# Mixer products cut at half a tile, more buffers in three pools, and a new work list for two transformer layers

## The chip, the core and the metric

The kernel runs on one core of a Trainium2 chip. TensorE (PE) multiplies matrices, VectorE (DVE), ScalarE (ACT) and GpSimd (POOL) work on vectors, and SyncE (SP) issues the transfers. Each engine takes its instructions in a fixed order. The metric is the device time of the whole program in microseconds (us), lower is better.

## What is computed

Two layers of a diffusion backbone run over 512 latent tokens of width 1024, with 256 context tokens in front of them. Each layer has a mixer with three groups of heads (attention, retention, a state space recurrence called SSD) and an MLP with squared ReLU; only the latent tokens are the output, so layer 1 leaves out the context rows where it can.

```python
def trunk_layer(x, xc, mod, mod_c, norm_g, w_in, w_out, ...):
    h = rmsnorm(x, norm_g[0]) * (1 + sc1[:, None]) + sh1[:, None]
    qa, ka, va, qr, kr, vr, gr, z, xbc, dt = jnp.split(h @ w_in, split_idx, axis=-1)
    att, att_c = attention_mixer(...)          # 6 query heads, 2 key heads, rotary
    ret, ret_c = retention_mixer(...)          # 4 heads, both directions, group norm, silu gate
    ssd, ssd_c = ssd_mixer(...)                # conv of 5 taps, silu, 6 heads, both directions, gated norm
    o = jnp.concatenate([att, ret, ssd], axis=-1) @ w_out
    x = x + g1[:, None] * rmsnorm(o, norm_g[1])
    h2 = rmsnorm(x, norm_g[2]) * (1 + sc2[:, None]) + sh2[:, None]
    x = x + g2[:, None] * rmsnorm(jnp.square(jax.nn.relu(h2 @ w1)) @ w2, norm_g[3])
    return x, xc
```

## The kernel before

Tokens stand in six tiles of 128 (four latent, two of context), and the model width in KC = 8 blocks of 128. Every large product is made of three matmuls (`mm3`): each operand is kept as a high part, rounded to the matmul's type, and a low part, the rest. So a weight piece (`wunit`) is loaded into a raw buffer `wr`, ACT writes its high part `wh` and DVE or POOL the low part `wl` (line 344); `h_h` and `h_l` (lines 570 and 571) are the same for the normed input, with POOL or DVE for `h_l`.

A layer runs in this order: the input norm, the convolution of xbc with SSD behind it, attention, retention, the output product, and the FF product, which is over half of the time. Layer 1's first input tiles are normed at the end of layer 0's FF (the layer boundary): `sandwich` scales the FF result (`tt`, `ors`, `xt`, lines 1489 to 1496), `norm_tile` transposes (`nps`) and modulates it; there POOL makes `h_l` and the low part of the first xbc weights, `wl_xbc`.

The mixers are written as some 250 named units, and `PLAN[l]` is a list of their names by hand; the loop at line 1414 calls them in that order. A scheduler then orders each engine's instructions by it, and by when buffers come free. The names: `kv` is the key, value and dt projection and `kp` its norm and rotary; `xw`, `xa`, `xb`, `xc`, `xt` are weight, first product, second product, taps and transposes of one of seven column blocks of the convolution; `qa`, `zz`, `kr`, `qg` are the other four projections, one unit a token tile; `f`, `m`, `b`, `g`, `sv`, `si`, `sd` belong to SSD (its `b` makes yi, for which POOL's `tb` is an input, and its `f` the product F from DVE's `gfb`); `as`, `at`, `ao` are attention's scores, transposes of P and products pv. In retention, of head h, `rl` loads the duplicated q and k (`ddqr`, `ddkr`), `rp` transposes them, `rx` centres v (`centre_v`), `rs` makes scores, `rd` the state sums, `rt` the states `rst` on DVE, `ro` the products `ry`, `rg` the gain on POOL, `rn` the group norm; `ur`, `us`, `ua` transpose the finished head groups into the mixer output (`sT`), and `wo` starts the output product (`op`) with the head groups that are ready.

Buffers: `t3` has four buffers and holds cin, acc and th of the convolution and other short-lived tiles, `m6` has three, the staging tiles `st` three. In the convolution ACT copies the product out of PSUM into `cin` (line 842), makes the first tap `acc` (line 850), DVE adds four taps (line 852), ACT takes the tanh `th` (line 854) and DVE the last product (line 861). POOL clears the edges of `cin` (lines 832 to 835) and, for qa, makes `wl_qa`. The gain tiles and `ry` of retention share two `m6` buffers, which `ret_y` takes once all of attention's products are done.

## Time and profile before

| what | value |
| --- | --- |
| median of 3 runs | 1861.27 us (1858.37 to 1863.56) |
| the profiled execution's own time | 1859.15 us |
| its span, first to last instruction | 1857.4 us |
| mean granted clock of TensorE | 0.972 |
| busy: PE, DVE, ACT, POOL | 1752.8, 1207.3, 703.0, 370.4 us |

Times in the views count from the span's start. A busy time is the sum of an engine's instructions; the idle time of PE in a stretch is the stretch less its busy time. PEclk is the granted clock as a share of 2.4 GHz, so 0.5 is 1.2 GHz. `[2.00 <-DMA ddqr]` behind a row says that the engine sat idle for 2.00 us before it and what ended that. "x4" merges four instructions in a row. In layer 0 the mixer takes the time from about 43 to 450 us, the output product that to 546 and FF that to 1088; layer 1's mixer runs from 1114 to 1447, and its FF from 1511 to the end.

### The profile page before, as it was taken

The page shows a single profiled execution, that of the slowest core. Times are in us where ns is not written, and L with a number is a line of the kernel's source. Part 1 is how long each engine was busy: PE and PEld are TensorE (multiplying, and loading weights), DVE is VectorE, ACT ScalarE, POOL GpSimd, SP SyncE. Part 2 cuts the span into 40 slices and gives each one's busy share as a digit, 9 for nine tenths or more (in the row PEclk, how much of TensorE's full clock was granted, in tenths as well). Part 3 has the DMA queues.
Part 4 walks back from the last instruction along what each step waited for, and adds up shares of the span by engine and source line. Part 5 has one row for each costly group of instructions (what it writes and reads, how often), then busy time and mean ns, then how long its engine had stood idle before and what let it go on. Part 6 is the DMA issues. An engine that isn't in the chain of part 4 may idle for free. (4 is left out here: it accounts for less than half of the span.)

```text
span 1857.4 us, 24648 instructions
## 1 busy us (share of the span) xinstructions
PE 1752.8 (94%) x8991; PEld 1440.8 (78%) x8991; DVE 1207.3 (65%) x2462; ACT 703.0 (38%) x1267; POOL 370.4 (20%) x391
## 2 busy tenths in 40 slices
PE   7998999998999999999999979899988999999998
PEld 2887977646878888888888878787767788888886
DVE  5878875776667566667556678788766644444445
ACT  6544376743551211211211475445751632222222
POOL 0047222313000100100100132543122011111112
PEclk9999999999999999999999989999985999999999
DMA  8420443466434434434434433133342522223332
GB/s 278 125 58 27 127 120 105 125 193 176 160 130 121 147 91 125 136 107 121 130 98 125 143 120 109 54 102 112 92 119 54 171 102 91 91 92 101 98 106 92
DMA packets 189077, 217.00 MB, mean 117 GB/s; under 512 B 67666, under 2 KB 142236, under 8 KB 188956
## 3 DMA queue, kind: packets, MB, share of 16 engines
q1 hardware_dynamic: 188956, 215.43, 38.9%
q8 instruction: 71, 1.16, 0.3%
q14 instruction: 50, 0.41, 0.1%
HBM read 189.66 MB, written 25.72 MB: 116 GB/s over the span
## 5 line engine op out<-in xcount | busy, mean ns | idle before, releaser
L589 PE MATMUL f<-h_h,wh_f 128*128 128x512 f32 (+1 forms) x800 | 280.6, 351 | 1.4 <-ACT h_h L570 1.4
L591 PE MATMUL f<-h_h,wl_f 128*128 128x512 f32 (+1 forms) x800 | 281.7, 352 | 0.0
L590 PE MATMUL f<-h_l,wh_f 128*128 128x512 f32 (+1 forms) x800 | 280.9, 351 | 0.8 <-DVE h_l L571 0.8
L1558 POOL TENSOR_TENSOR r<-r 128x768 f32<-128x768 f32 (+1 forms) x64 | 95.7, 1496 | 841.1 <-ACT r L1557 734.3
L589 PE MATMUL f<-wh_g,uh 128*128 128x512 f32 x640 | 252.7, 395 | 2.5 <-DVE uh L1559 1.6
L590 PE MATMUL f<-wl_g,uh 128*128 128x512 f32 x640 | 252.5, 395 | 0.0
L591 PE MATMUL f<-wh_g,ul 128*128 128x512 f32 x640 | 251.8, 393 | 0.0
L343 ACT ACTIVATE wh_f<-wr_f 128x1024 fp32r<-128x1024 f32 x64 | 66.5, 1055 | 374.5 <-PE f L591 133.1
L1588 DVE TENSOR_TENSOR acc<-acc,f 128x512 f32<-128x512 f32 x140 | 96.1, 686 | 121.0 <-PE f L591 119.6
L589 PEld LDWEIGHTS f<-h_h,wh_f 128*128 128x128 f32 x800 | 152.4, 191 | 23.1 <-ACT h_h L570 1.5
L590 PEld LDWEIGHTS f<-h_l,wh_f 128*128 128x128 f32 x800 | 151.6, 190 | 22.9 <-DVE h_l L571 1.0
L591 PEld LDWEIGHTS f<-h_h,wl_f 128*128 128x128 f32 x800 | 151.8, 190 | 20.8
L527 DVE SCALAR_TENSOR_TENSOR ga<-wr_mg,cg_a,ga 128x512 f32<-128x512 f32 x216 | 151.2, 752 | 12.5 <-DMA wr_mg<-in_w_mod_dram 12.4
L589 PEld LDWEIGHTS f<-wh_g,uh 128*128 128x128 f32 x640 | 120.1, 188 | 31.5 <-DVE uh L1559 2.1
L591 PEld LDWEIGHTS f<-wh_g,ul 128*128 128x128 f32 x640 | 120.2, 188 | 28.6
L590 PEld LDWEIGHTS f<-wl_g,uh 128*128 128x128 f32 x640 | 120.2, 188 | 27.3
L1557 ACT ACTIVATE r<-f 128x768 f32<-128x768 f32 (+1 forms) x64 | 44.6, 697 | 193.5 <-PE f L591 126.6
L1559 DVE CAST uh<-r 128x768 fp32r<-128x768 f32 (+1 forms) x64 | 32.4, 506 | 126.3 <-POOL r L1558 126.3
L344 DVE TENSOR_TENSOR wl_f<-wr_f,wh_f 128x1024 fp32r<-128x1024 f32 x64 | 77.6, 1221 | 50.8 <-ACT wh_f L343 50.7
L344 DVE TENSOR_TENSOR wl_g<-wr_g,wh_g 128x1024 fp32r<-128x1024 f32 x62 | 75.4, 1222 | 51.4 <-ACT wh_g L343 51.4
L343 ACT ACTIVATE wh_g<-wr_g 128x1024 fp32r<-128x1024 f32 x64 | 67.3, 1056 | 94.2 <-DMA wr_g<-in_w_ff_dram 55.5
L589 PE MATMUL xbc<-h_h,wh_xbc 128*128 128x512 f32 (+1 forms) x208 | 71.9, 346 | 3.9 <-ACT cin L842 3.9
(405 smaller groups left out, 3762.2 us busy)
## 6 DMA issues: line engine op xcount, KB each, us to landing
wr_f<-in_w_ff_dram SPq DMA_DIRECT2D x64, 512.0 KB
wr_g<-in_w_ff_dram SPq DMA_DIRECT2D x64, 512.0 KB
wr_mg<-in_w_mod_dram SPq DMA_DIRECT2D x192, 128.0 KB
wr_m<-in_w_mod_dram SPq DMA_DIRECT2D x24, 512.0 KB
m<-in_w_mod_dram SPq DMA_DIRECT2D x32, 256.0 KB
wr_o<-in_w_out_dram SPq DMA_DIRECT2D x16, 512.0 KB
wr_xbc<-in_w_in_dram SPq DMA_DIRECT2D x14, 512.0 KB
xmid<-xt SPq DMA_DIRECT2D x10, 512.0 KB
```

The lines of the kernel that those rows point to most:

```text
L343: S.activation(hv[:, a0 : a0 + an], r, AF.Copy)
L344: (lo_eng or V).tensor_tensor(lv[:, a0 : a0 + an], r, hv[:, a0 : a0 + an].bitcast(F32), ALU.subtract)
L527: V.scalar_tensor_tensor(acc[:, s], r2[:, k % 2], w, acc[:, s], ALU.mult, ALU.add)
L589: T.matmul(o, a[0], b[0], start=first, stop=False)
L590: T.matmul(o, a[0], b[1], start=False, stop=False)
L591: T.matmul(o, a[1], b[0], start=False, stop=last)
L1557: S.activation(r, q[:, :NT], AF.Relu)
L1558: G.tensor_tensor(r, r, r, ALU.mult)
L1559: V.tensor_copy(uh, r)
L1588: V.tensor_tensor(acc[tt][:, ns], acc[tt][:, ns], qs[tt][half], ALU.add)
```

## The change

The products of `xa`, `qa`, `zz`, `kr` and `qg` are divided into two units at KC/2 (`xa3.` and `xa3`). The scratch of the dynamic DMAs is set to 2048 bytes a partition; `t3` goes from four to six buffers, `m6` and `st` from three to four. `ret_y` is gone: `ry` and the gain tiles are t3 tiles. `rv` (the load of v for retention) depends on `kr5` alone. `wo` has nine units for six, and a unit `wq` loads another weight piece for them. Low parts move: of the eight `wl_qa` and of the two `wl_xbc` of the boundary from POOL to DVE, of the last but one `h_l` there too, of one attention put (`ua2`) a layer and of one modulation piece, and one skip product a layer. Three modulate operations of a tile go from DVE to ACT (CUT). Both lists are new; of them the diff shows the first rows of layer 1's.

```diff
-ATT_N9 = True
+ATT_N9 = False
+KNOBS = dict(
+    H_LO="GGGGVV", KV_LATE=1, X_LO="VVVVVVVV", W_LO="VVVVVVVV", P_MUL="VSVSVS", SKIP="VVGVGV",
+    U_LO="GGV", MOD="GGGVGG", T3=6, M6=4, S1=3, ST=4, CUT="443444",
+)
...
     1: """
-        kv0 kv1 kv2 kv3 kv4 kv5 km0 km1 xw3 xa3 xb3 xa4 xc3 xb4 xt3 xc4 xw5 xa5 kp1 xc5 de xa6 xt4
...
+        kv0 kv1 kv2 kv3 kv4 kv5 km0 km1 xw3 xa3. xa3 xb3 xa4. xa4 xb4 xc3 xt3 xw5 xa6. xa5. xc4 kp1 xa5 xt4 de
...
-        modulate(q, xh.rearrange("p (k t) -> p k t", k=KC), tt, l, which, hT, lo_eng)
+        modulate(q, xh.rearrange("p (k t) -> p k t", k=KC), tt, l, which, hT, lo_eng, (0, KC), int(KNOBS["CUT"][tt]))
...
-        t3 = lambda shape, name, dt=F32: mp.tile(shape, dt, tag="t3", name=f"{name}{l}", bufs=4)
+        t3 = lambda shape, name, dt=F32: mp.tile(shape, dt, tag="t3", name=f"{name}{l}", bufs=KNOBS["T3"])
-        m6 = lambda shape, name, dt=F32: mp.tile(shape, dt, tag="m6", name=f"{name}{l}", bufs=3)
+        m6 = lambda shape, name, dt=F32: mp.tile(shape, dt, tag="m6", name=f"{name}{l}", bufs=KNOBS["M6"])
...
-        def tm_group(name, n, cols, nt, consume, banks=(pB,), us=None):
-            us = us or [wunit(wcols(w_in[l], 4 * u, cols), (128, 4, n), f"{name}{l}{u}", G if name == "qa" else None) for u in range(2)]
+        def tm_group(name, n, cols, nt, consume, banks=(pB,), us=None, split=False):
+            us = us or [wunit(wcols(w_in[l], 4 * u, cols), (128, 4, n), f"{name}{l}{u}", eng(KNOBS["W_LO"][4 * l + ("qa", "zz", "kr", "qg").index(name)]) if not us else None) for u in range(2)]
...
+                    if split and k == KC // 2 - 1:
+                        yield
...
+                if k == KC // 2 - 1 and part == 0:
+                    yield
...
-            for t in range(nt):
-                unit(f"{nm}{t}", steps(gen), f"{nm}{t - 1}" if t else "kv5")
+            for t in range(nt):
+                unit(f"{nm}{t}.", steps(gen), f"{nm}{t - 1}" if t else None)
+                unit(f"{nm}{t}", steps(gen), f"{nm}{t}.")
...
-        def ret_y():
-            RV["y"] = [m6([128, 1536], f"ry{i}") for i in range(2)]
...
-                ry[pr] = RV["y"][pr][:, :768].rearrange("p (t h d) -> p t h d", t=6, h=2)
+                ry[pr] = t3([128, 6, 2, 64], f"ry{pr}")
...
-            a, b = (RV["y"][h % 2][:, c : c + 384].rearrange("p (t d) -> p t d", d=64)[:, :NQ] for c in (768, 1152))
+            ab = t3([128, 2, 6, 64], f"gg{h}")
+            a, b = ab[:, 0, :NQ], ab[:, 1, :NQ]
...
-        unit("rv", ret_v, "kr5", *[f"at{h}{t}" for h in range(6) for t in range(NQ)])
-        unit("ryt", ret_y, *[f"ao{h}{t}" for h in range(6) for t in range(NQ // 2)])
+        unit("rv", ret_v, "kr5")
...
-            WP["g"] = wout_begin(l, MX["m"], WP["p"], 6)
+            WP["g"] = wout_begin(l, MX["m"], WP["p"], 9)
+
+        def wo_more():
+            WP["p"][0][1, 1] = wout_unit(l, 1, 1)
...
-                    kvw.append(xbc_unit(l + 1, (3, 4), G))
+                    kvw.append(xbc_unit(l + 1, (3, 4), eng(KNOBS["X_LO"][4])))
...
-    nc = bacc.Bacc("TRN2", target_bir_lowering=False, num_devices=1)
+    nc = bacc.Bacc("TRN2", target_bir_lowering=False, num_devices=1, dynamic_dma_scratch_size=2048)
```

On DVE, at the layer boundary, where `xt` of one tile is followed by the modulate operations of the next (lines of the changed kernel are about 54 lower). Before:

```order
L1491 TENSOR_TENSOR tt_9702<-acc05_5369,gr011_9611 128x512
L299 SCALAR_TENSOR_TENSOR rm_t_9557<-nrs_9554,rm_h_9556 128x1
L299 SCALAR_TENSOR_TENSOR rm_t_9625<-ors_9618,rm_h_9624 128x1
L303 SCALAR_TENSOR_TENSOR nrs_9554<-rm_t_9557,nrs_9554 128x1
L303 SCALAR_TENSOR_TENSOR ors_9618<-rm_t_9625,ors_9618 128x1
L1495 SCALAR_TENSOR_TENSOR xt_9613<-tt_9614,ors_9618,xt_9613 128x1024
L1492 TENSOR_TENSOR oss_9705<-oss_9705 128x1
```

After:

```order
L233 SCALAR_TENSOR_TENSOR rm_t_9629<-ors_9622,rm_h_9628 128x1
L233 SCALAR_TENSOR_TENSOR rm_t_9561<-nrs_9558,rm_h_9560 128x1
L237 SCALAR_TENSOR_TENSOR ors_9622<-rm_t_9629,ors_9622 128x1
L1437 TENSOR_TENSOR tt_9706<-acc05_5373,gr011_9615 128x512
L237 SCALAR_TENSOR_TENSOR nrs_9558<-rm_t_9561,nrs_9558 128x1
L1441 SCALAR_TENSOR_TENSOR xt_9617<-tt_9618,ors_9622,xt_9617 128x1024
L278 TENSOR_TENSOR wl_xbc13_9696<-wr_xbc13_0_9697,wh_xbc13_9695 128x1024
L278 TENSOR_TENSOR wl_xbc13_9696<-wr_xbc13_4_9701,wh_xbc13_9695 128x1024
```

The two `wl_xbc`, which POOL made before, stand behind `xt`.

On PE, at the end of layer 1's attention, from its last pv on. Before:

```order
L1176 MATMUL pv151_12584<-PT5101_12547,vat1_11263 128x256 x6
L1176 MATMUL pv151_12584<-PT5111_12548,vat1_11263 128x256 x6
L274 MATMUL dTqr01_12621<-ident_69,ddqr01_12606 128x128 x4
L1280 MATMUL rd10_12666<-vrr1_12603,W01_12477 128x64 x6
L1273 MATMUL rs100_12688<-qT01_12627,kT01_12626 128x128 x4
L274 MATMUL dTkr11_12646<-ident_69,ddkr11_12639 128x128 x4
L1304 MATMUL ry10_12711<-vrr1_12603,W01_12477 128x64
L274 MATMUL dTqr11_12651<-ident_69,ddqr11_12640 128x128 x4
L1305 MATMUL ry10_12711<-rst10_12694,q201_12628 128x64
L1304 MATMUL ry10_12711<-vrr1_12603,W01_12477 128x64
```

After, from one row earlier:

```order
L208 MATMUL pt1531_12586<-ident_69,P531_12575 128x128 x3
L1122 MATMUL pv151_12592<-PT5101_12555,vat1_11362 128x256 x6
L1122 MATMUL pv151_12592<-PT5111_12556,vat1_11362 128x256 x6
L1223 MATMUL rd10_12656<-vrr1_12461,W01_12439 128x64 x6
L208 MATMUL dTkr11_12663<-ident_69,ddkr11_12649 128x128 x4
L208 MATMUL dTqr11_12668<-ident_69,ddqr11_12650 128x128 x4
L1216 MATMUL rs100_12704<-qT01_12631,kT01_12630 128x128 x4
L1223 MATMUL rd11_12710<-vrr1_12461,W11_12644 128x64 x3
L208 MATMUL sT15_12688<-ident_69,fr01_12686 128x128 x4
L1223 MATMUL rd11_12710<-vrr1_12461,W11_12644 128x64 x2
L208 MATMUL sT16_12697<-ident_69,fr11_12695 128x128 x4
L1223 MATMUL rd11_12710<-vrr1_12461,W11_12644 128x64
```

The transposes of `ddqr` of head 0 and the two transposes of head 1 stand earlier, and the sums rd of head 1 with two sT stand ahead of head 0's `ry`.

On DVE, at the same place, from the last attention products on. Before:

```order
L1180 TENSOR_TENSOR fo511_12597<-fo511_12597,pv151_12584 64x256
L1342 TENSOR_REDUCE mu10_12612<-vrr1_12603 128x6
L1342 TENSOR_REDUCE mu11_12662<-vrr1_12603 128x6
L1343 TENSOR_SCALAR mu10_12612<-mu10_12612 128x6
L1343 TENSOR_SCALAR mu11_12662<-mu11_12662 128x6
L1344 TENSOR_TENSOR vrr1_12603<-vrr1_12603,mu10_12612 128x6x64
L1344 TENSOR_TENSOR vrr1_12603<-vrr1_12603,mu11_12662 128x6x64
L1249 TENSOR_TENSOR q201_12628<-dTqr01_12621,W01_12477 128x512
L1293 COPY rst10_12694<-rd10_12666 64x64 x2
L1295 SCALAR_TENSOR_TENSOR rst10_12694<-rst10_12694,g1281_9794,rd10_12666 64x64 x2
```

After:

```order
L1288 TENSOR_TENSOR vrr1_12461<-vrr1_12461,mu12_12796 128x6x64
L1287 TENSOR_SCALAR mu13_12855<-mu13_12855 128x6
L278 TENSOR_TENSOR wl_o111_13072<-wr_o111_0_13073,wh_o111_13071 128x1024
L1126 TENSOR_TENSOR fo501_12551<-fo501_12551,pv150_12538 64x256
L1113 TENSOR_TENSOR PT5101_12555<-pt1520_12557,PT5101_12555 128x3x128
L1288 TENSOR_TENSOR vrr1_12461<-vrr1_12461,mu13_12855 128x6x64
L278 TENSOR_TENSOR wl_o111_13072<-wr_o111_2_13077,wh_o111_13071 128x1024
L1113 TENSOR_TENSOR PT5111_12556<-pt1521_12563,PT5111_12556 128x3x128
L1113 TENSOR_TENSOR PT5101_12555<-pt1530_12580,PT5101_12555 128x3x128
L1195 TENSOR_TENSOR q201_12632<-dTqr01_12625,W01_12439 128x512
L1113 TENSOR_TENSOR PT5111_12556<-pt1531_12586,PT5111_12556 128x3x128
L1126 TENSOR_TENSOR fo511_12605<-fo511_12605,pv151_12592 64x256
```

The centring of v (`mu`, `vrr`) and two `wl_o` stand among attention's `PT` operations, ahead of the last `fo`.

## Rows read from the trace of the kernel before

**Rows 1.** The page, section 1: busy time, share of the span and instructions of PE.

```profile
PE 1752.8 (94%) x8991; PEld 1440.8 (78%) x8991; DVE 1207.3 (65%) x2462; ACT 703.0 (38%) x1267; POOL 370.4 (20%) x391
```

**Rows 2.** Stretches: length; busy us of PE, PEld, DVE, ACT, POOL; PEclk; DMA share; GB/s.

```profile
43.00:230.00 187.00, 175.46 (x1056) 159.55 (x1057) 155.56 (x402) 87.18 (x180) 72.57 (x95) 0.99 0.29 85
385.00:450.00 65.00, 55.82 (x309) 34.00 (x308) 40.97 (x115) 19.91 (x35) 16.42 (x17) 0.95 0.70 197
1165.00:1270.00 105.00, 95.20 (x537) 86.74 (x538) 86.65 (x218) 43.00 (x82) 52.48 (x56) 0.97 0.31 90
1270.00:1380.00 110.00, 101.36 (x583) 81.71 (x581) 83.16 (x176) 80.30 (x162) 23.72 (x36) 0.97 0.32 94
1380.00:1447.00 67.00, 55.09 (x239) 48.32 (x238) 41.36 (x131) 13.99 (x28) 14.59 (x14) 0.59 0.29 72
```

**Rows 3.** Waits of PE: engine, tile and line waited for; us in total, times, longest.

```profile
PE nps L274 <- ACT tt L576: 10.1, 2, 7.8
...
PE ry L1305 <- DVE rst L1295: 9.0, 4, 5.5
PE yi L940 <- POOL tb L931: 6.2, 3, 2.7
PE xbc L589 <- ACT cin L842: 3.9, 3, 2.0
...
PE xt L274 <- DVE th L861: 3.9, 4, 1.4
PE qap L589 <- ACT cin L842: 3.4, 2, 2.8
...
PE F L914 <- DVE gfb L898: 3.1, 2, 1.8
...
PE kvp L591 <- POOL h_l L571: 1.9, 1, 1.9
```

**Rows 4.** Timeline, layer boundary, POOL and DVE: start, us, engine, line, operation, tiles.

```profile
1088.47 2.43 POOL L344 TENSOR_TENSOR wl_xbc<-wr_xbc,wh_xbc 128x1024 fp32r<-128x1024 f32 x1
...
1088.58 3.40 DVE L1495 SCALAR_TENSOR_TENSOR xt<-tt,ors,xt 128x1024 f32<-128x1024 f32 x1
...
1094.62 2.88 POOL L344 TENSOR_TENSOR wl_xbc<-wr_xbc,wh_xbc 128x1024 fp32r<-128x1024 f32 x1 [3.72 <-ACT wh_xbc L343]
...
1095.22 2.29 DVE L299 SCALAR_TENSOR_TENSOR rm_t<-nrs,rm_h 128x1 f32<-128x1 f32 x1
1097.43 0.21 DVE L299 SCALAR_TENSOR_TENSOR rm_t<-ors,rm_h 128x1 f32<-128x1 f32 x1
...
1097.87 1.28 DVE L1495 SCALAR_TENSOR_TENSOR xt<-tt,ors,xt 128x1024 f32<-128x1024 f32 x1
```

**Rows 5.** Timeline, layer 0's convolution: DVE's taps, POOL's wl_qa, ACT's tanh.

```profile
105.83 4.45 DVE L852 SCALAR_TENSOR_TENSOR acc<-cin,pcol,acc 128x772 f32<-128x772 f32 x4
...
117.70 1.85 POOL L344 TENSOR_TENSOR wl_qa<-wr_qa,wh_qa 128x768 fp32r<-128x768 f32 x1 [0.72 <-ACT wh_qa L343]
...
118.81 3.75 DVE L852 SCALAR_TENSOR_TENSOR acc<-cin,pcol,acc 128x772 f32<-128x772 f32 x3
...
122.59 0.85 ACT L854 ACTIVATE th<-acc 128x772 f32<-128x772 f32 x1 [4.97 <-DVE acc L852]
```

**Rows 6.** Line 344 by form: ns min/median/max, first and last start.

```profile
L344 DVE TENSOR_TENSOR wl_zz<-wr_zz,wh_zz x8: 944/959/2041, 134.6 to 1218.3; 128x768 fp32r<-128x768 f32 x8
```

**Rows 7.** Timeline, layer 1's retention, on PE and DVE.

```profile
1382.20 0.63 PE L274 MATMUL dTqr<-ident,ddqr 128*128 128x128 f32 x4 [2.00 <-DMA ddqr<-qrd]
...
1390.73 1.01 DVE L1342 TENSOR_REDUCE mu<-vrr 128x6 f32<-128x384 f32 x2
...
1408.34 1.49 DVE L1326 TENSOR_TENSOR ry<-ry 128x256 f32<-128x256 f32 x1
...
1421.42 0.42 DVE L1326 TENSOR_TENSOR ry<-ry,ry 128x256 f32<-128x256 f32 x1
...
1440.89 0.39 PE L1305 MATMUL ry<-rst,q 128*128 128x64 f32 x2
```

More of the change, by code (lines that the diff above doesn't have):

```diff
@@ L590, in mm3 @@
         T.matmul(o, a[0], b[1], start=False, stop=False)
-        T.matmul(o, a[1], b[0], start=False, stop=last)
+        return T.matmul(o, a[1], b[0], start=False, stop=last)
     xmid = [dp.tile([TOK, D], F32, name=f"xmid{l}") for l in range(DEPTH)]
@@ L724, in mixers, with kv_step @@
         kv_gen = tm_group("kv", 268, [(KA, 0, 256), (DT0, 256, 12)], 6, c_kv, (pB, pC), kvw[:1])
+        def kv_step(t):
+            if l and t < KNOBS["KV_LATE"]:
+                with tc.issue_after(last_ff2[0].ins):
+                    next(kv_gen, 0)
+            else:
+                next(kv_gen, 0)
         for t in range(6):
-            unit(f"kv{t}", steps(kv_gen), f"kv{t - 1}" if t else None)
+            unit(f"kv{t}", lambda t=t: kv_step(t), f"kv{t - 1}" if t else None)
         def kv_move(i):
@@ L828, in conv_in @@
             if part == 0:
-                cins[j] = t3([128, 776], "cin")
-            cin = cins[j]
-            if part == 0:
+                cin = cins[j] = t3([128, 776], "cin")
                 G.memset(cin[:, 0:2], 0.0)
@@ L1642, in start @@
         big9 = [mp.tile([128, 2304], F32, tag="n9", name=f"x9{i}", bufs=2) for i in range(2)]
-        big6 = [mp.tile([128, 1536], F32, tag="m6", name=f"x6{i}", bufs=3) for i in range(2)]
+        big6 = [mp.tile([128, 1536], F32, tag="m6", name=f"x6{i}", bufs=KNOBS["M6"]) for i in range(2)]
         xT = [b[:, o : o + D] for b, o in ((big9[0], 0), (big9[0], D), (big9[1], 0), (big9[1], D), (big6[0], 0), (big6[1], 0))]
```

193 lines of the change are left out of this document (66 added, 127 removed).

## Prediction

> **What bounds the kernel now.** I read the page's busy times first. TensorE (PE) is busy for 94% of the span [rows 1], so a shorter kernel can come only out of PE's idle time, some 95 us if the gaps above 0.1 us are added up, or out of the clock that it works at. Next I read the table of stretches [rows 2], where PE's idle time is the length less its busy time: 11.5 us in layer 0's convolution and SSD (43 to 230), 9.2 us in layer 0's retention (385 to 450), 9.8 us in layer 1's SSD (1165 to 1270), 8.6 us in layer 1's attention, and 11.9 us in layer 1's retention (1380 to 1447). This last one is the worst place for a second reason: its granted clock is 0.59, so most of it ran at 1.2 GHz and not at 2.4. Its 55.1 us of PE work would take about 55.1 x 0.59 = 33 us at the high level. VectorE (DVE) is busy for 83% of the stretches 43 to 230 and 1165 to 1270 and for 62% of the retention, so it is the engine next behind PE. The waits of PE by cause come third [rows 3]; the five rows in it with cin, th, tb and gfb are the convolution and SSD, 20.5 us together. Last I read the order of time at the three places below. The long FF stretches have next to no idle time and are barely touched; I cost them at nothing.
>
> **The layer boundary.** While GpSimd (POOL) makes wl_xbc in 2.43 and 2.88 us, DVE's small operations stand still [rows 4]: the 128x1 operation at 1095.22 takes 2.29 us and ends with POOL's (1097.50), while the same form right behind it takes 0.21; xt takes 3.40 us at 1088.58 and 1.28 at 1097.87. That is 2.1 us twice. The chain rm_t, nrs, tt, nps stands behind the second, and PE waits 7.8 us for tt [rows 3]. The change puts both wl_xbc on DVE, 1.28 us each by the 0.96 that it takes for three quarters of that size [rows 6], and they stand behind xt and ahead of the next tile's four modulate operations. So 4.2 us of stretch go and 2.6 come, part of both beside other waits: between 1.6 and 4.2, and I take 3. The last h_l but one also goes from POOL to DVE, and PE's 1.9 us for POOL's h_l [rows 3] shrinks by some 1. The sum is **4** us, bounds 0 and 6.
>
> **Convolution and SSD of both layers.** ScalarE works in order, and its copy cin of the next projection, which frees the PSUM bank for PE, stands behind a tanh that waits for DVE's taps: at 122.59 ACT had waited 4.97 us for them [rows 5]. More t3 slots (six for four) let cin, acc and th of a second column block be made earlier, the half units let PE go over to another product within a tile, and POOL, which also clears cin, loses eight wl_qa of 1.85 us. On the other side DVE gets these eight at 0.96 us [rows 6], 3.8 us in each layer, and one more skip operation. The taps show what it gets back: three of them beside POOL's wl_qa took 3.75 us, four with no wl_qa about took 4.45 and so three 3.34 [rows 5]. One overlap of 0.74 us (118.81 to 119.55) thus cost 0.41. If every wl_qa gives back only 0.4 us, the move is a loss of 8 x (0.96 - 0.4) = 4.5 us of DVE time; if every one had blocked DVE for its whole 1.85, a gain of 8 x (1.85 - 0.96) = 7.1. I take 0 for this. The Trainium skill, "SBUF — State Buffer", section "Who interferes with whom", says that an operation of DVE with two inputs in SBUF contends with GpSimd's reads, as an exclusive lock. By that the upper end would hold and the sum would be 7 us better; the boundary's rows agree with a full lock, the taps' row shows about half of one. Of the 20.5 us of waits I let half go, **10** us: the cause of the cin and th waits (11.2 us) is met directly, while yi, which waits for POOL's tb, and F, which waits for gfb, only get more PE work ahead of them. Bounds 0 and 18.
>
> **Layer 0's retention.** One transposed retention pair (sT) moves between the scores and sums of head 2, and three output products move ahead of the last scores; I let a third of its 9.2 us go, **3** us, bounds -1 and 6.
>
> **Layer 1's retention.** Before, some 61 us lie between the end of the last pv (2.00 us before 1382.20) and that of head 3's last ry products, 1441.3 [rows 7]. The change does four things. The load of ddqr and of vrr and the centring of v by DVE come ahead of the last pv, so that the 2.0 us for ddqr [rows 7] and the centring pairs, of which the first reduction alone is 1.01 us for two [rows 7] and all twelve operations 4.7 us, leave this chain. The sums rd of head 1 and two transposes are put between the sums of head 0 and its ry products, which waits for DVE's rst; such waits were 9.0 us in four, the longest 5.5 [rows 3]. The gain products of POOL use other slots; where they ran, a 128x256 operation of DVE took 1.49 us, and the same form 0.42 later [rows 7]. And ry of head 0 and 1 is transposed (sT13) ahead of head 2's sums, where it waits for head 1's norm. This last is a new wait: some seventeen tiny operations, at most 0.21 us each by [rows 4], and three of 0.42 stand on DVE in front of it, below 5 us, with about 5 us of PE's transposes and scores as cover at the low clock and half of that at the high one; I put 1 to 2.5 us on it. DVE's rst of head 1 stays interleaved with the norm of head 0, so about 4 us of waiting remain there.
> With the clock low throughout, the chain is 49 us of PE's work (61 less 11.9 idle), less 1.5 for a transpose moved out and fewer output products, plus 4 and 1: 52 us, a gain of 9. With the clock high, PE's share is about 26 us and DVE's work becomes the bound: 41.4 us [rows 2] less 4.7 of centring and some 2 of stretch, plus short waits, 35 to 38 us: a gain of 23. The clock was low right behind the gap of 2.0 us, which the change removes, but the 4 us at head 1's rst are longer than that. I take the middle, **16** us.
>
> **The ends of attention pay for it.** 4.7 us of centring, 0.6 of decay and two wl_o of 1.28 stand among DVE's attention operations now, 7.9 us against 26.8 us of DVE's idle time in 1270 to 1380 [rows 2]; the vector work on PT that they are put between is what pv waits for. I take **-3** us for both layers, bounds -7 and 0.
>
> **What I cost at nothing or in the lump.** The DMA scratch: the page lists no packets of a software queue, only hardware ones, so I see nothing that uses it. The three modulate operations that go to ACT and the wl of one modulation piece lie beside FF products. Layer 1's list is rewritten in every line, and new short waits at joints that I haven't costed are as likely as the ones that I saw; five of 1 us, **-5** us, bounds -12 and 0.
>
> **The sum.** 4 + 10 + 3 + 16 - 3 - 5 = 25 us against the profiled execution's 1859.15, so 1834. The median of the runs is 2.1 us above that execution, which gives 1836 as the time to expect.
>
> **The rivals.** (1) The tail's clock stays high. For it: the gap in front of its fall goes. Against: 4 us of waiting inside it. It gives 7 us more, and if every wl_qa had blocked DVE for its whole length, or conv's waits all went, 7 more: 1822 to 1829. (2) The clock stays low throughout and the conv waits come back at other joints: gains of 9 in the tail and 3 in the conv stretches, so 1836 + 7 + 7 = 1850. For it: DVE is at 83% there and gets more work. (3) The list doesn't matter, because the engines' queues and the slots set when things start: the waits stay where they were, 1861. Against it stands that PE's own queue is reordered around the very waits of [rows 3], and PE is in order. (4) Slower: DVE becomes the bound. It gets 8 x 0.96 + 2 x 1.28 + 1.3 + 0.7 us = 12 in the conv stretches and the boundary, and 7.9 at each end of attention; if nothing of that is hidden, 28 us are lost, against 9 in the tail, 3 in layer 0's retention and 4 of relief at the boundary: 1861 + 12 = 1873. It decides from the point at which DVE has no idle time left ahead of the taps and of PT; it had 31.4 us of it in 43 to 230 and 18.3 in 1165 to 1270 [rows 2], which speaks against it.
>
> **How the numbers follow.** The forecast (both clocks in the tail, half of the conv waits gone; 1827 to 1845) gets 0.5, (1) 0.15, (2) 0.18, (3) 0.08 and (4) 0.09. The range reaches from inside (1), 1816, to 1857, which takes in (2): it leaves out little of (1) and all of (3) and (4). About 0.3%, 5.6 us, is what a measurement of this kernel can tell from no change; faster than 1855.7 are the forecast, (1) and nearly all of (2).
>
> **What would show it.** Right: PEclk of the 60 us behind the last pv above 0.65, ry waiting for rst below 6 us in total, no wait of PE for ddqr there; nps waiting at most 5 us; xbc and qap waiting for cin below 3.5 us together; POOL without wl_qa and wl_xbc, and DVE without operations of 128x1 above 1 us at the boundary. Wrong: PE waiting for wl_qa or PT in new rows of more than 2 us, a wait of sT for ry above 4 us, or the tail still at 0.6 of the clock and as long as before.

## The result, and the profile after

The kernel after takes 1831.66 us (median of 4 runs, 1831.06 to 1833.8), the kernel before in the same comparison 1862.41 (1858.37 to 1865.6). The ratio is 0.9838 with a 95% interval of 0.9816 to 0.986: 30 us faster, 5 more than the forecast and inside its range. The profiled execution of after took 1831.16 us, its span is 1829.4 and its mean granted clock 0.979.

The busy line of the page, as [rows 1]:

```profile
PE 1737.7 (95%) x8991; PEld 1433.7 (78%) x8991; DVE 1208.8 (66%) x2474; ACT 701.7 (38%) x1270; POOL 342.4 (19%) x376
```

PE's idle time, span less busy, went from 104.6 to 91.7 us, and its busy time fell by 15.1 although the number of its instructions is the same. Much of that second part is the clock: at a share c, the time at 1.2 GHz is 2 x (1 - c) of the stretch, by the mean clocks 104 us before and 77 after. Each us of PE's work in it costs half. Added up from the traces, PE was busy for 78.4 us at the lower level before and for 58.9 after, so the clock is worth 9.7 us of the 28.0 by which the span fell.

The stretches that answer to [rows 2], by the same columns, with the stage borders of after:

```profile
43.00:230.00 187.00, 175.42 (x1063) 160.98 (x1061) 159.85 (x409) 88.98 (x185) 67.97 (x88) 0.98 0.29 86
...
1160.00:1253.00 93.00, 86.71 (x506) 79.36 (x507) 83.66 (x219) 42.52 (x83) 38.13 (x41) 1.00 0.33 96
1253.00:1365.40 112.40, 104.35 (x597) 85.99 (x595) 91.85 (x194) 82.83 (x166) 30.45 (x39) 0.95 0.39 110
1365.40:1407.00 41.60, 34.27 (x202) 31.46 (x202) 29.46 (x104) 8.70 (x18) 8.88 (x11) 0.75 0.44 106
```

Layer 1's retention, from the last pv to the last ry of head 3, takes 41.6 us for 61.1, with 7.3 us of PE's idle time and a clock of 0.75. With the same borders in both traces (first kvp and first scores `s` of each layer, last ry, first and last FF product), the whole span divides so:

| stage | before, us | after, us | difference | of it products that crossed a border | rest | forecast |
| --- | --- | --- | --- | --- | --- | --- |
| start, to the first kvp | 43.2 | 45.5 | +2.3 | +2.9 | -0.6 | 0 |
| layer 0: convolution and SSD | 188.9 | 183.5 | -5.4 | -3.2 | -2.2 | -5 (half of 10) |
| layer 0: attention and retention | 230.5 | 227.5 | -3.0 | +1.2 | -4.2 | -3 + 1.5 |
| layer 0: output product and FF | 623.0 | 628.5 | +5.5 | -0.9 | +6.4 | 0 |
| boundary, to the last kvp | 37.7 | 34.5 | -3.2 | +2.2 | -5.4 | -4 |
| layer 1: convolution and SSD | 147.4 | 133.9 | -13.5 | -4.7 | -8.8 | -5 (half of 10) |
| layer 1: attention | 109.6 | 112.0 | +2.4 | +3.4 | -1.0 | +1.5 |
| layer 1: retention | 61.1 | 41.6 | -19.5 | -1.8 | -17.7 | -16 |
| layer 1: output product and FF | 416.1 | 422.4 | +6.3 | +0.9 | +5.4 | 0 |

The new list lets some products of PE stand in another stage than before, so a difference is not all gain or loss. Eight `mq` (modulation) run ahead of the first kvp and no longer behind it, eleven `xbc` ahead of the last kvp, ten `krp` (of kr), four `dTqr` and two `rd` come into layer 1's attention, one `krp` comes into layer 0's, and four `op` of each layer change sides at the last ry. The fifth column prices them by PE's busy time on them in the two traces (2.9 us for the eight `mq`, 2.2 for the eleven `xbc`, about 0.25 for one `krp` or `op`); "rest" is what is left. Each column comes from one execution of each kernel, and a stage differs by some us between executions of the same code, layer 1's retention by 5 (below).

So without these products 39 us were won at the places for which the forecast had 33 less 3, and the two stretches with FF took 12 back where it put a lump of 5. One edit, the switch `KV_LATE`, is explained neither with the change nor in the forecast: the first `kv` tile of layer 1 is held behind layer 0's last FF product. PE starts it at the end of that product in both traces (1085.4 us before, 1084.9 after), so none of this is its doing.

PE's waits by cause, as [rows 3]:

```profile
PE nps L208 <- ACT tt L510: 9.2, 4, 3.9
PE sT L208 <- DVE ry L1269: 4.7, 2, 3.3
PE yi L885 <- POOL tb L876: 4.5, 1, 4.5
PE ry L1248 <- DVE rst L1238: 3.8, 2, 3.5
PE pt L208 <- DVE PT L1113: 3.7, 4, 1.8
...
PE gps L208 <- DVE mc L356: 2.8, 1, 2.8
...
PE qap L523 <- ACT cin L785: 2.0, 1, 2.0
...
PE kvp L525 <- POOL h_l L505: 1.9, 1, 1.9
...
PE f L523 <- DVE acc L1532: 1.9, 1, 1.9
PE xbc L523 <- ACT cin L785: 1.9, 2, 1.5
...
PE sT L208 <- DMA fr<-ssdd: 1.5, 1, 1.5
...
PE xt L208 <- DVE th L804: 1.4, 1, 1.4
...
PE F L859 <- DVE gfb L843: 0.9, 1, 0.9
```

ry waits for rst 3.8 us in place of 9.0, xt for th 1.4 for 3.9, xbc and qap for cin 3.9 together for 7.3, F for gfb 0.9 for 3.1. yi (one wait of 4.5) and nps (four for two) remain, kvp's 1.9 for POOL's `h_l` is as it was, and the 2.0 us for ddqr are gone. New are the waits of the transposes `pt` for DVE's PT, 3.7 us in four (0.2 before), of which 2.9 are at the end of layer 1's attention, where the centring was put.

**The boundary**, as [rows 4]; the timeline of POOL:

```profile
1085.95 3.36 POOL L505 TENSOR_TENSOR h_l<-tt,h_h 128x1024 fp32r<-128x1024 f32 x1 [0.90 <-ACT h_h L504]
```

The timeline of DVE:

```profile
1086.97 2.35 DVE L1438 TENSOR_TENSOR oss<-oss 128x1 f32<-128x1 f32 x1
...
1092.02 0.22 DVE L233 SCALAR_TENSOR_TENSOR rm_t<-nrs,rm_h 128x1 f32<-128x1 f32 x1
...
1092.90 1.28 DVE L1441 SCALAR_TENSOR_TENSOR xt<-tt,ors,xt 128x1024 f32<-128x1024 f32 x1
1094.09 2.36 DVE L278 TENSOR_TENSOR wl_xbc<-wr_xbc,wh_xbc 128x1024 fp32r<-128x1024 f32 x2
```

With `wl_xbc` on DVE (2.36 us for two), rm_t takes 0.22 us and xt 1.28, where they took up to 2.29 and 3.40. One 128x1 operation still takes 2.35 us: it lies beside POOL's last `h_l` and ends with it. The wait of nps here went from 7.8 to 3.9 us, and PE's time at the low clock in this stage from 10.2 to 3.4.

**The retention on PE**, as [rows 7]; the first row stands right behind the last pv, with no wait:

```profile
1365.22 1.45 PE L1223 MATMUL rd<-vrr,W 128*128 128x64 f32 x12
...
1380.10 0.69 PE L1248 MATMUL ry<-rst,q 128*128 128x64 f32 x2 [3.53 <-DVE rst L1238]
...
1386.52 1.09 PE L208 MATMUL sT<-ident,fr 128*128 128x128 f32 x4 [1.46 <-DMA fr<-ssdd]
...
1389.55 1.11 PE L208 MATMUL sT<-ident,ry 128*128 128x128 f32 x4
...
1397.35 0.78 PE L523 MATMUL op<-wh_o,mix_h 128*128 128x512 f32 x1
```

A pair of `ry` products that takes 0.39 us up to 1373.8 takes 0.63 from 1380.6 on: the clock fell to its lower level inside the 3.53 us for rst of head 1, at 1378.8. It rose again at 1399.3, 2 us into the 512-column output products `op`. Between these stands a wait that the forecast didn't have, 1.46 us for the transfer of `fr` (SSD's result, which `sT` transposes). The transposes of `ry` at 1389.55 wait for nothing.

**The start of layer 1's FF**, where time was given back; the timeline of POOL:

```profile
1454.22 4.75 POOL L278 TENSOR_TENSOR wl_g<-wr_g,wh_g 128x1024 fp32r<-128x1024 f32 x2 [43.03 <-ACT wh_g L277]
```

Of DVE:

```profile
1455.28 1.36 DVE L233 SCALAR_TENSOR_TENSOR rm_t<-ors,rm_h 128x1 f32<-128x1 f32 x1
1456.68 2.31 DVE L237 SCALAR_TENSOR_TENSOR ors<-rm_t,ors 128x1 f32<-128x1 f32 x1
```

Of PE:

```profile
1465.45 1.76 PE L208 MATMUL nps<-ident,tt 128*128 128x128 f32 x7 [3.26 <-ACT tt L510]
```

POOL makes the two `wl_g` in one piece of 4.75 us, and DVE's tiny operations on `ors`, through which the next normed tile has to go, take 1.36 and 2.31 us beside it. PE then waits 3.26 us, and its clock is low for 6.8 us from that wait on. In the kernel before the same two `wl_g` lay 2.6 us apart and the two `ors` operations fell between them; its timeline of POOL:

```profile
1481.23 3.47 POOL L344 TENSOR_TENSOR wl_g<-wr_g,wh_g 128x1024 fp32r<-128x1024 f32 x1 [56.02 <-ACT wh_g L343]
1487.31 3.20 POOL L344 TENSOR_TENSOR wl_g<-wr_g,wh_g 128x1024 fp32r<-128x1024 f32 x1 [2.61 <-ACT wh_g L343]
```

And of DVE:

```profile
1486.51 0.22 DVE L299 SCALAR_TENSOR_TENSOR rm_t<-ors,rm_h 128x1 f32<-128x1 f32 x1
1486.77 0.16 DVE L303 SCALAR_TENSOR_TENSOR ors<-rm_t,ors 128x1 f32<-128x1 f32 x1
```

No edit touches these instructions. It isn't the new list that makes them meet: in the run with the old lists below the two `wl_g` lie in one piece too (1491.14 to 1495.90), and in that with the moves alone, on the kernel before, they lie apart. Which of the other edits it is, the nine units of `wo` or the buffers among them, wasn't settled.

### The profile page after: what moved, and what is told of

Its sections match the earlier page's. It is cut to its first block, busy times and chain, and to the rows that moved or that the text cites. A ratio compares the mean times of both kernels' runs of the same rounds, so it can differ in the third digit from the quotient of the medians.

```text
span 1829.4 us, 24602 instructions
## 1 busy us (share of the span) xinstructions
PE 1737.7 (95%) x8991; PEld 1433.7 (78%) x8991; DVE 1208.8 (66%) x2474; ACT 701.7 (38%) x1270; POOL 342.4 (19%) x376
## 5 line engine op out<-in xcount | busy, mean ns | idle before, releaser
L461 DVE SCALAR_TENSOR_TENSOR ga<-wr_mg,cg_a,ga 128x512 f32<-128x512 f32 x216 | 153.7, 764 | 15.2 <-DMA wr_mg<-in_w_mod_dram 15.1
```

Source lines behind the costliest of these rows:

```text
L461: V.scalar_tensor_tensor(acc[:, s], r2[:, k % 2], w, acc[:, s], ALU.mult, ALU.add)
```

## The experiments

The theory was the forecast's: the new list carries the gain, most of all by keeping PE's clock up in layer 1's retention, and the moves of low parts and the buffers are small beside it. The rival was that POOL's low parts, which hold DVE up, matter as much, whatever the list. Each kernel is compared with the kernel before on the same chip; the size of an effect is read against the 1831.66 us of after. The letters A and B are those of each run's own expectation.

### All moves of low parts undone

```diff
-    H_LO="GGGGVV", X_LO="VVVVVVVV", W_LO="VVVVVVVV", SKIP="VVGVGV", U_LO="GGV", MOD="GGGVGG", CUT="443444",
+    H_LO="GGGGGV", X_LO="VVVVGVVV", W_LO="GVVVGVVV", SKIP="GVGVGV", U_LO="GGG", MOD="GGGGGG", CUT="444444",
```

> The changed kernel with all work that went from POOL to DVE (eight wl_qa, two wl_xbc, one h_l, one skip product and one attention put a layer, one modulation piece) put back on POOL, and the modulate operations back on DVE; list, half units and slots stay. Theory A (the list and the slots carry the gain; the moves give the layer boundary and nothing net in the convolution): 1836 us, 1832 to 1841, the boundary's nps wait back near 7 us. Theory B (freeing DVE from POOL's locks carries it): 1845 us or more, with the waits for cin and th back at 10 us.

1846.78 us (1842.1 to 1850.6), ratio 0.9911 (0.9885 to 0.9936): 15 us slower than after, as B said. By stage against after: layer 0's convolution +3.7, the boundary +2.7 (+4.9 without the eleven `xbc`, which stand behind it here), layer 1's convolution +6.5, its attention +3.0, its retention +6.4, while layer 0's output product and FF are some 4 us shorter. PE's waits for th and cin are 9.6 us in all (5.3 in after), and nps waits 7.8 us at the boundary again. So the moves are worth half of the gain as things stand. That they also help the retention, in which only one put went back to POOL, isn't shown: it ran 36.7 us at the low clock instead of 20.5, but the same code as in after did so for 34.1 us in the execution of the run with `wl_g` on DVE.

### The old lists under everything else

```diff
-        kv0 kv1 kv2 kv3 kv4 kv5 km0 km1 xw3 xa3. xa3 xb3 xa4. xa4 xb4 xc3 xt3 xw5 xa6. xa5. xc4 kp1 xa5 xt4 de
+        kv0 kv1 kv2 kv3 kv4 kv5 km0 km1 xw3 xa3. xa3 xb3 xa4. xa4 xc3 xb4 xt3 xc4 xw5 xa5. xa5 kp1 xc5 de xa6. xa6 xt4
...
```

> The changed kernel with the two lists of before (each half unit stands right in front of its other half, the three new output units and wq at the end); slots, engine moves and the new dependencies stay. Theory A (the list carries the gain, above all layer 1's retention): 1853 us, 1846 to 1858, the 60 us behind the last pv at a clock of about 0.6 again. Theory B (slots and engine moves carry it): 1836 us, 1832 to 1841, with the tail's clock at 0.75 or more.

1864.69 us (1859 to 1867), ratio 1.0011 (0.9998 to 1.0023). The whole gain is gone, 33 us and more than A expected. The retention (columns as [rows 2]) is as it was:

```profile
1383.20:1444.20 61.00, 48.07 (x207) 42.97 (x208) 37.46 (x121) 11.02 (x22) 12.75 (x13) 0.55 0.32 77
```

61.0 us at a clock of 0.55. That is 19.4 of the 33; layer 1's attention is another 6.7 (118.7 us), with 9.7 us in nine waits of the scores for their exponentials. Attention took 109.6 in before, and it takes 111.2 on this list with the moves alone (below), so neither the list nor the moves by themselves make it worse. What does, of buffers, two half units in a row and new dependencies, wasn't settled. Together they cost under the old list: the moves alone gain 5.5 us on it, and with all the rest nothing is gained.

### Whole units for the halves

```diff
-                unit(f"{nm}{t}.", steps(gen), f"{nm}{t - 1}" if t else None)
+                unit(f"{nm}{t}.", lambda: None, f"{nm}{t - 1}" if t else None)
-            gen = tm_group(nm, n, cols, nt, consume, split=True)
+            gen = tm_group(nm, n, cols, nt, consume, split=False)
...
```

> The changed kernel with each product whole again: the first half unit does nothing, the second does the whole tile at its place in the new list. Theory A (half units only shift a wait by half a tile): 1834 us, 1831 to 1838. Theory B (the half tiles are what fills PE's waits in convolution and SSD): 1842 us or more, with the cin, th, yi and F waits 8 us higher.

1836.4 us (1834.3 to 1838.6), ratio 0.9856 (0.9836 to 0.9876): 5 us slower (the fastest of its four runs is 0.5 us behind the slowest of after), inside the range that A gave. The division that names the change is worth little beside its list.

### The load and centring of v late again

```diff
-... ao41 rv ...
-... rl0 rx0 rp0 rx1 ...
+... ao41 ...
+... rl0 rv rx0 rp0 rx1 ...
```

> The changed kernel with one name of layer 1's list moved: rv, the load of v for retention, stands behind the last pv and not among the last attention heads, so the centring of v falls back behind the last pv. Theory A (the gap behind the last pv makes the clock fall and this costs most of the tail's gain): 1842 us, 1838 to 1847, PEclk of the 42 us behind the last pv near 0.6. Theory B (what counts is that head 1's sums stand ahead of head 0's ry): 1834 us, 1831 to 1836, a wait of 2 to 3 us for v alone and the clock as it is.

1843.13 us (1839.5 to 1846.6), ratio 0.9886 (0.9861 to 0.9911): 11.5 slower, as A said. The retention takes 54.6 us; its row of the stretches:

```profile
1367.70:1422.30 54.60, 43.14 (x207) 39.30 (x206) 35.91 (x116) 10.12 (x20) 11.68 (x12) 0.62 0.40 97
```

PE's first sums behind the last pv:

```profile
1371.39 2.80 PE L1223 MATMUL rd<-vrr,W 128*128 128x64 f32 x12 [3.21 <-DVE vrr L1288]
```

The sums `rd`, which in after follow the last pv at once, wait 3.21 us for the centred v, and the same twelve take 2.80 us where they took 1.45: the clock falls at the head of the retention and stays low for 41 of the 54.6 us. Against after's own 41.6 us this one unit's place is worth 13 us of the retention, against the 46.9 of the run with `wl_g` on DVE 8.

### wl_qa back on POOL, alone

```diff
-    W_LO="VVVVVVVV",
+    W_LO="GVVVGVVV",
```

> The changed kernel with the eight wl_qa alone back on POOL. Theory A (what DVE gets back from POOL's locks equals the 0.96 us that each costs it): 1832 us, 1829 to 1835. Theory B (each of POOL's 1.85 us locks DVE fully, and the taps are the path): 1839 us or more, taps of 1.1 us stretched to 2 or 3 beside POOL's wl_qa, and waits for cin or th longer by 4 us or more.

1851.52 us (1848.7 to 1853.6), ratio 0.994 (0.9923 to 0.9956): 20 us slower, as B said. The forecast had put 0 on this move. DVE's timeline in after, four taps of the convolution:

```profile
125.71 4.26 DVE L795 SCALAR_TENSOR_TENSOR acc<-cin,pcol,acc 128x772 f32<-128x772 f32 x4
```

The same in this kernel:

```profile
118.77 7.28 DVE L795 SCALAR_TENSOR_TENSOR acc<-cin,pcol,acc 128x772 f32<-128x772 f32 x4
...
129.69 5.86 DVE L795 SCALAR_TENSOR_TENSOR acc<-cin,pcol,acc 128x772 f32<-128x772 f32 x4 [1.70 <-ACT acc L793]
```

And POOL's timeline beside it:

```profile
117.93 2.59 POOL L278 TENSOR_TENSOR wl_qa<-wr_qa,wh_qa 128x768 fp32r<-128x768 f32 x1
...
120.69 2.35 POOL L278 TENSOR_TENSOR wl_qa<-wr_qa,wh_qa 128x768 fp32r<-128x768 f32 x1
127.81 3.68 POOL L278 TENSOR_TENSOR wl_qa<-wr_qa,wh_qa 128x768 fp32r<-128x768 f32 x2 [4.76 <-ACT wh_qa L277]
```

In the kernel before there is such a pair as well; its timeline of DVE:

```profile
126.62 5.84 DVE L852 SCALAR_TENSOR_TENSOR acc<-cin,pcol,acc 128x772 f32<-128x772 f32 x4 [2.19 <-ACT acc L850]
```

And of POOL:

```profile
124.74 3.66 POOL L344 TENSOR_TENSOR wl_qa<-wr_qa,wh_qa 128x768 fp32r<-128x768 f32 x2 [5.08 <-ACT wh_qa L343]
```

Four taps take 4.26 us with POOL quiet. The first four of the run share 1.75 us with one `wl_qa` (118.77 to 120.52) and 2.35 with the next, 4.10 in all, and take 3.02 us longer; the second four share 1.80 us with the third row and take 1.60 longer, and those of the kernel before share 1.78 and take 1.58 longer. In these last two DVE lost all of the overlap but 0.20 us. In the first four the second `wl_qa` began beside a tap that was already running, and there POOL lost: it took 2.35 us for the 1.85 of the quiet ones. Both operations of [rows 4] fit too: xt lost 2.12 us of 2.32, rm_t 2.08 of 2.28. The forecast had read 0.41 in 0.74 out of [rows 5]; but the 4.45 us that it took for four quiet taps have other operations of POOL (`kvt`, `rp`) beside them, and by 4.26 the loss is 0.55, again the overlap less 0.2. The Trainium skill, "SBUF — State Buffer", section "Who interferes with whom", calls this an exclusive lock; these rows agree with it but for the 0.2 us.

By stage it costs 4.1 us in layer 0's convolution, 10.3 in layer 1's (9.3 without four `krp`, which stand in attention in after), 4.2 in its attention and 5.2 in its retention; the last is no more than the same code differs by between executions. DVE's own time explains little of it. Seven of its operations lost 10.8 us beside the eight `wl_qa`, by their times against those of the same form elsewhere, and DVE is spared 7.7, a net of 3. The rest are waits behind the taps that were held up, and the row of PE's waits that grew most shows them, 8.1 us for 1.4 in after:

```profile
PE xt L208 <- DVE th L804: 8.1, 3, 4.4
```

This one move seems to cost more than undoing it together with all the others (15 us), but the two intervals overlap (0.9923 to 0.9956, 0.9885 to 0.9936), so that isn't shown.

### wl_g of layer 1's FF on DVE

```diff
-    ... G if b == 0 and l in (1,) and v == 0 else None
+    ... None
```

> The changed kernel with one more move: the low part of the first two output weight pieces of layer 1's FF (two wl_g, 2.4 us each) goes from POOL to DVE. Theory A (these two lock DVE while the tiny operations rm_t and ors stand ahead of xt, so PE's 3.3 us for nps at 1465 and the low clock of 6.8 us behind it come from POOL): 1826 us, 1823 to 1829, with the wait for nps there below 1.5 us. Theory B (2 x 1.22 us more on DVE delay the same chain): 1832 us, 1830 to 1835.

1829.14 us (1827.1 to 1835.1), ratio 0.9826 (0.9804 to 0.9847): 2.5 less than after, with intervals that overlap. The local effect is plain. The two `ors` operations in DVE's timeline, as above:

```profile
1464.11 0.21 DVE L233 SCALAR_TENSOR_TENSOR rm_t<-ors,rm_h 128x1 f32<-128x1 f32 x1
...
1465.38 0.15 DVE L237 SCALAR_TENSOR_TENSOR ors<-rm_t,ors 128x1 f32<-128x1 f32 x1
```

0.21 and 0.15 us, PE's 3.26 us and the low clock behind it are gone, and layer 1's FF takes 363.3 us for 367.2 in after (361.1 in before). That settles the cause of most of what was given back there. The profiled execution is the slowest of the four, 1835.1 us: it lost 5.3 us in the retention (columns as [rows 2]), where nothing differs from after:

```profile
1367.90:1414.80 46.90, 38.67 (x203) 35.52 (x202) 29.56 (x103) 8.82 (x18) 9.70 (x11) 0.64 0.38 95
```

Its clock fell at 1373.7, behind a wait of `rd` for DVE's W of 1.45 us. After has the same wait, 1.45 us up to 1370.07, and there the clock held until 1378.8. So the same code spends 20.5 or 34.1 us of the retention at the low clock, and a difference of 5 us there between two kernels shows nothing by itself.

### rst of head 1 ahead of head 0's norm

```diff
-... ro00 ro01 rn0 rw2 rl2 rp2 rx2 rs1 rt1 ro10
+... ro00 ro01 rt1 rn0 rw2 rl2 rp2 rx2 rs1 ro10
```

> The changed kernel with one name of layer 1's list moved: rt1, the states of head 1, stands ahead of rn0, the norm of head 0, so that DVE makes rst without the norm's operations in between. Theory A (the 3.5 us for rst and the clock that falls behind it are DVE's order): 1825 us, 1820 to 1828, no wait for rst above 1.5 us, PEclk of the 42 us behind the last pv at 0.85 or more. Theory B (the wait only goes over to the transposes of head 0 and 1's result, whose norm is then later): 1831 us, 1829 to 1834, sT waiting 2 to 4 us for ry.

1830.69 us (1829.9 to 1831.2), ratio 0.9828 (0.9811 to 0.9844): no change. The wait for rst is gone, and another has come in its place, in PE's timeline:

```profile
1386.28 1.09 PE L208 MATMUL sT<-ident,fr 128*128 128x128 f32 x4 [3.89 <-DMA fr<-ssdd]
```

`sT` now waits 3.89 us for the transfer of `fr`. It starts within 0.3 us of where it started in after, since that transfer is issued no earlier (1383.41 us, and 1383.65 in after). The retention takes 44.0 us at a clock of 0.69. Half of B came true: the wait went on, though not to the one that it named.

### t3 with four buffers

```diff
-    T3=6, M6=4,
+    T3=4, M6=4,
```

> The changed kernel with four t3 buffers for six (m6 and st keep four); list, halves and moves stay. Theory A (the convolution's and the retention's order needs the slots): 1840 us, 1834 to 1848, with waits for cin and th 5 us higher and new waits in layer 1's retention, where ry and the gain tiles are t3 tiles. Theory B (the order alone carries the gain): 1832 us, 1830 to 1834.

1854.35 us (1851.7 to 1862.6), ratio 0.9965 (0.9949 to 0.9982): 23 slower, more than A's 1834 to 1848. From PE's waits by cause (us in total, times, longest), the largest that after doesn't have:

```profile
PE dTqr L208 <- DMA ddqr<-qrd: 5.5, 1, 5.5
PE F L859 <- DVE gfb L843: 5.3, 1, 5.3
PE xt L208 <- DVE th L804: 4.7, 3, 4.3
```

Layer 0's convolution takes 15.2 us more (F for gfb 5.3 us, xt for th 4.3 at the longest), layer 1's 6.9, the retention 8.2 (ddqr 5.5). Of these, 2.9 us are the eight `mq`, which stand behind the first kvp here, and 3.5 of layer 1's are fourteen `krp` that stand in attention in after. The list needs the two buffers. Fewer `m6` buffers weren't tried.

### The moves alone, on the kernel before

```diff
-            ... f"{name}{l}{u}", G if name == "qa" else None) ...
+            ... f"{name}{l}{u}", None) ...
-                (G, V)[t % 2].tensor_tensor(v3(y_tok[:, t]), ...)
+                (V, V, G, V, G, V)[t].tensor_tensor(v3(y_tok[:, t]), ...)
-            put(j, f[:, :NT], None, G)
+            put(j, f[:, :NT], None, (G, G, V)[j])
-                    kvw.append(xbc_unit(l + 1, (3, 4), G))
+                    kvw.append(xbc_unit(l + 1, (3, 4), V))
-                              hTn if wc else None, G if tt < NQ - 1 else V, ...)
+                              hTn if wc else None, G if tt < (NQ - 2 if wc else NQ - 1) else V, ...)
...
```

> The kernel before with the engine moves alone (eight wl_qa, two wl_xbc, the last but one h_l, a skip product and an attention put a layer and one modulation piece to DVE, one tile's modulate cut); old lists, old buffers, whole tiles. Theory A (the moves pay only where list and slots let the convolution's taps run ahead; on the old list the boundary alone gains): 1856 us, 1851 to 1860, layer 1's retention as long and at as low a clock as before. Theory B (what POOL's locks cost is there under any order): 1847 us or less.

1855.24 us (1850.5 to 1865), against 1860.71 for before in this comparison; ratio 0.9969 (0.9944 to 0.9993): a gain of 5.5, as A said. The boundary shortens by 1.8 us, layer 0's convolution by 1.6 and layer 1's by 4.7; as in after eleven `xbc` of 2.2 us have gone over from the last to the first, so by work it is 4.0, 1.6 and 2.5, and the boundary isn't alone. The retention shortens, by the columns of [rows 2], not at all:

```profile
1376.10:1437.40 61.30, 49.40 (x211) 43.75 (x211) 39.12 (x123) 11.73 (x24) 12.96 (x13) 0.55 0.31 76
```

So the moves are worth 5.5 us on the kernel before and 15 on the changed one; list, buffers and halves differ between the two together.

### The DMA scratch alone, on the kernel before

```diff
-    nc = bacc.Bacc("TRN2", target_bir_lowering=False, num_devices=1)
+    nc = bacc.Bacc("TRN2", target_bir_lowering=False, num_devices=1, dynamic_dma_scratch_size=2048)
```

> The kernel before with the scratch of the dynamic DMAs at 2048 bytes and nothing else. Theory A (nothing uses it): 1862 us, within 0.2% of before. Theory B (fewer descriptors in flight slow the transfers): 1867 us or more, with longer waits for DMA in the first 43 us.

1859.77 us, ratio 0.9986 (0.9973 to 0.9999). Less than 0.3%: the smaller scratch costs nothing.

### The retention's two waits taken out, with wl_g on DVE

```diff
-... ro00 ro01 rn0 rw2 rl2 rp2 rx2 rs1 rt1 ro10
+... ro00 ro01 rt1 rn0 rw2 rl2 rp2 rx2 rs1 ro10
-... rx3 us2 ur0 rd2 rw3 rl3 rp3 ... rt2 wp rd3
+... rx3 rd2 rw3 rl3 rp3 us2 ... rt2 wp rd3 ur0
-    ... G if b == 0 and l in (1,) and v == 0 else None
+    ... None
```

> The changed kernel with three changes of place in layer 1's list (rt1 ahead of rn0; us2, the third transposed SSD group, and ur0, the transposes of head 0 and 1's result, behind the sums of heads 2 and 3) and with the two wl_g of layer 1's FF on DVE. Theory A (the waits for rst, fr and ry are each a matter of what stands ahead in an in-order queue): 1822 us, 1817 to 1827, the stretch between the last pv and the last ry at 36 us or less, PEclk there above 0.85. Theory B (the engines' total work in the tail sets it, so a wait removed comes back elsewhere): 1829 us, as with the move of wl_g alone.

1829.87 us (1827.7 to 1830.9), ratio 0.9826 (0.9806 to 0.9847): 2 us below after, with overlapping intervals, as B said. The retention and a stretch inside it, by the columns of [rows 2]:

```profile
1364.80:1403.80 39.00, 35.42 (x197) 32.37 (x197) 28.52 (x104) 8.85 (x18) 9.28 (x11) 0.69 0.46 113
1372.00:1393.00 21.00, 19.23 (x86) 17.79 (x86) 15.48 (x61) 4.50 (x11) 5.64 (x6) 0.50 0.57 134
```

Of PE's timeline:

```profile
1369.48 0.85 PE L1223 MATMUL rd<-vrr,W 128*128 128x64 f32 x6 [1.45 <-DVE W L1217]
...
1396.00 0.50 PE L523 MATMUL op<-wh_o,mix_h 128*128 128x512 f32 x1 [0.36 <-DVE mix_l L1304]
```

PE's idle time fell to 3.6 us (7.3 in after), and the retention takes 39.0 for 41.6, of which 1.1 are five `op` that stand behind it here. But the clock didn't stay high. It fell at 1371.2, behind the 1.45 us wait of the first row of PE. From 1372 to 1393 PE is busy for 19.23 of 21.00 us and the granted clock is 0.50 all that time; it rose at 1395.1, under small products still: the second row is the first of 512 columns. Taking the last waits out thus gave 3.7 us of idle time, and 23.9 us at the low clock for 20.5, PE busy for 22.1 of them against 17.8, took 2.2 back. The wait behind which the clock fell stands in after too, and it fell behind it in the run with `wl_g` on DVE as well, so these 2.2 us are not the list's doing.

### wl_g, the last h_l but two and the modulation pieces

```diff
-    H_LO="GGGGVV", MOD="GGGVGG",
+    H_LO="GGGVVV", MOD="GGGGGG",
-    ... G if b == 0 and l in (1,) and v == 0 else None
+    ... None
```

> The changed kernel with the two wl_g of layer 1's FF and the h_l of the boundary's fourth tile on DVE too, and the modulation piece back on POOL. Theory A (each removes the wait that the trace names: 3.3 us for nps at 1465, 1.9 for h_l at 1104, 2.8 for gps at 904): 1824 us, 1820 to 1828. Theory B (the boundary's DVE chain gets longer by 1.2 us and the other two are covered by the next wait): 1829 us, 1827 to 1832.

1833.85 us (1831.4 to 1836.3), ratio 0.9849 (0.9827 to 0.9872): no gain over after, and above the ranges of both A and B. kvp's 1.9 us for `h_l` is gone and a wait of 1.4 us for `h_h`, ACT's part of the same tile, has come instead. FF of layer 1 is 4 us shorter, as with wl_g alone. gps in layer 0's FF still waits 2.1 us with all modulation pieces on POOL, so that piece's move isn't what it waits for.

No kernel here beats after by more than the runs can tell.

## Why the prediction was right, and which terms weren't

**The boundary** (4, bounds 0 and 6): 5.4 us without the products that crossed the border, by the mechanism that it gave. 6.8 us less at the low clock came on top, which it hadn't counted; the 1 us for kvp's wait for `h_l` did not come, it is 1.9 as before. It overlooked that `h_l` on POOL still meets DVE: one operation of 2.35 us remains.

**Convolution and SSD** (10, bounds 0 and 18): 18.9 us by the borders, 11 without the products that crossed them. The size was right. The named waits shrank as it said, xbc and qap for cin by 3.4 us of 7.3, xt for th by 2.5 of 3.9, F by 2.2; yi only changed from three waits to one, 1.7 us less. The reason was wrong: the 10 were to come from list, slots and half units, with `wl_qa` at 0. With `wl_qa` alone on POOL these stages are 13 us longer than in after, and with all moves undone 10 (both without the products that crossed), so without the moves next to nothing of the 11 is left. The step that failed is to price `wl_qa` in DVE's own time and apart from the list. In that time the 0 was close, although the loss of 0.41 in 0.74 under it was misread: in the kernel before seven operations of DVE lost 8.1 us beside the eight `wl_qa`, which take 7.7 on DVE. What it left out is what waits behind a tap that is held up by 1.6 us: th, and PE's transposes of it. That the 10 fit is luck in this respect. The second error is to have summed the edits one by one. On the kernel before the moves bring 5.5 us, on the changed one 15; the changed kernel without the moves still brings 15.7, without the wider t3 7, with the old lists nothing. A part of the change can't be given a price of its own here.

**Layer 0's attention and retention** (-1.5 net): -3.0, or -4.2 without the products that crossed, inside the bounds. Some of the retention's work went into attention (12.2 us longer, and the rest 15.1 shorter), which the forecast had not seen in that size.

**Layer 1's retention** (16, between 9 with the clock low and 23 with it high): 19.5, and by the mechanism given. The time at the low clock, 2 x (1 - c) of the stretch as above, fell from 54.6 to 20.5 us; PE was busy for 44.8 and 17.8 of these, so that is worth 13.5 us. 4.6 us of idle time went, and 1.8 of work moved out (1.5 forecast). It had "about 4 us" left for rst of head 1, and it is 3.53. The new wait of `sT` for `ry` that it put at 1 to 2.5 us does not exist, and a wait of 1.46 for the transfer of `fr`, which it hadn't looked at, does. Late centring alone costs 11.5 us, so "the gap in front of its fall goes" was the part that mattered most. The number owes something to the execution: a middle between two cases was forecast, and the same code gives 14 us in the execution of the run with `wl_g` on DVE and 19.5 here.

**The ends of attention** (-3 for both layers): the +2.4 us in layer 1 are products that moved in (3.4 us); without them the stage is 1.0 shorter. PE does wait 2.9 us more for PT there, as feared, but other waits went. In layer 0 no loss can be told apart.

**Costed at nothing, and the lump of 5**: the start's +2.3 are the eight `mq`, and PE is idle there for 12.9 us after 13.4. The two long stretches with FF (+5.5 and +6.3) gave back 12 us, for which the forecast was too kind. Layer 1's is shown for the most part: the two `wl_g` on POOL met the norm's small operations, with 3.26 us of waiting and 6.8 at the low clock, and 3.9 us come back with `wl_g` on DVE. Layer 0's is not: gps waits 2.8 us for DVE's `mc` and f 1.9 for `acc`, but kernels with the same code there took between 558.6 and 564.0 us for that FF, so it hangs on small shifts of time.

So the total is right partly because two errors met: the places named gave 39 us for the 30 of their terms, and the FF stretches took back 12 for the lump of 5. Of the rivals, (1) was half true (the clock is at 0.75, neither low throughout nor high) and its lock of POOL on DVE true but for 0.2 us an operation, (2) and (3) fell with the stretches above, and (4) by the run with `wl_qa` on POOL: taking work off DVE there makes the kernel slower. The range's lower end, 1816, is called inside (1) and lies below its 1822.

Of the signs named: PEclk above 0.65 (0.75 over the 41.6 us of the retention), ry's wait below 6 us (3.8), no wait for ddqr and POOL without `wl_qa` and `wl_xbc` came true; nps at most 5 us (9.2, of which 3.9 at the boundary), cin below 3.5 (3.9) and no long 128x1 operation at the boundary did not. Two signs of being wrong came true in total, neither with one long wait: pt waits 3.7 us for PT (the longest 1.8), and sT 4.7 us for ry (3.3 and 1.4, both in layer 0; 2.6 before).

**What stays open**: what delays layer 0's FF, which edit made the two `wl_g` of layer 1's FF meet the norm, and what lets the clock rise inside the retention, or hold behind the same wait in one execution and not in another. `wo`, `wq`, and the wider `m6` and `st` were not taken out by themselves.
